# Weight pieces first in the schedule, and three pieces of VectorE's and GpSimd's work moved, in a hybrid block in float32

## The chip, the cores and the metric

The kernel runs on one core of one Trainium2 chip. The metric is the device time of one execution in microseconds, as a median of several; less is better. The core has five engines that matter here, each with its own instructions in a fixed order: TensorE (PE in the profile, PEld for its weight loads), VectorE (DVE), ScalarE (ACT), GpSimd (POOL) and SyncE (SP), which issues most DMAs.

## What is computed

One layer of a decoder block with two branches, for a sequence of 512 and a width of 1024:

```python
u = rmsnorm(x, norm1_g)
proj = u @ w_in       # conv channels of A, z, decay and beta; q, k, v of B; indexer; two gates
# A: gated delta rule, 8 heads, chunks of 64
g = -exp(a_log) * softplus(g_a + dt_bias)
q, k, v = silu(causal conv of width 4 over the channels); q, k normalised
T = inverse of (I + strictly lower (beta k k^T * decay));  then a loop over chunks with a state
# B: the indexer chooses 128 keys a query, 8 query heads attend to them
score = sum over 8 heads of iw * relu(iq . ik)       # causal
o = attention over the top 128 keys
m = sigmoid(gate_a) * A + sigmoid(gate_b) * B
h = x + m @ w_out
h = h + (silu(conv3(up_gate)) * conv3(up_val)) @ w_down     # up: 1024 to 2 x 2816
out = rmsnorm(h, final_g)
```

All inputs are float32.

## The kernel before

The large products are made of float32 parts. A weight comes in pieces of 512 KB ([128, 1024]) by `load`, from SP's queue into `raw`; `piece` then lets ScalarE cast it to the high part `whi` (line 196) and lets VectorE or GpSimd, as its argument says, subtract that from `raw` for the low part `wlo` (line 197). `raw`, `whi` and `wlo` have three buffers each. A product is three matmuls a step (`passes`, lines 200 to 206): high by low, low by high, high by high. Activations are split in the same way (`xgh` and `xgl`, `uTh` and `uTl`, `hTh` and `hTl`). Products are gathered in `acc`, a PSUM tile with three buffers; `channel_major` makes two of them, of 24 matmuls of 512 columns each, from two pieces. Its first argument is the engine for the first piece's low part, its third (GpSimd unless given) that for the second's.

The stages in order of time:

1. dv and the small products (decay, beta, indexer key and weights), from x times g; the row statistics `r4` come from the x tiles `xt`.
2. The indexer's queries: two calls of `channel_major` over `xg` give four accumulators, each cut in two halves; ScalarE copies a half to `iq` and VectorE subtracts it from the accumulator for the low half (line 432). In the meantime VectorE makes the indexer's key `ikn`, the decay chain (lines 383 to 397: `s0`, `s1`, `s2`, `gd`, all 128x32) and `uv`, the normalised x, with its low part `uTl` (lines 420 to 422). The chain's end `gd` is read by a cumulative sum on TensorE (`gp`, line 400).
3. Scores of query blocks 1 to 3, and the first half of branch A (`gdn_half(0)`: 4 heads): convolutions (`conv_silu`: ScalarE makes `y` out of an accumulator, three VectorE rows of line 462 add the shifted ones), the matrices `MT`, and the inverse. The inverse of the 32x32 blocks is a chain on VectorE: 30 steps of two rows, `tw` and `wi` (lines 585 and 587). Its result goes by DMA through memory back to `MT`, is transposed to `UT` (line 597), and products `m1` to `m4` (from line 603) join the blocks.
4. The top-k of each block on VectorE: 16 passes of MAX8 (line 690) and a replacement of the eight found (line 691) over 256, 384 and 512 columns; nothing but VectorE works at it, and its result is wanted by the attention in stage 6.
5. dk, dq, and the second half of branch A (`gdn_half(1)`).
6. Attention, z and the gates, W_out, the feed-forward: 22 chunks of two pieces, whose accumulators are read by ScalarE and twice by VectorE each (lines 896 and 898), then down and the last norm.

Nothing of this order is binding: the framework's scheduler writes every engine's instructions in an order of its own, by priority (the place in the program, unless code changes it) and by simulated readiness. `after(b, a)` makes it place b behind a, without a semaphore.

Of the kernel before, what the change touches and what calls it, by code (L numbers as in the profile page):

```python
# [9 lines left out]
F = mybir.dt.float32  # L10
# [3 lines left out]
OP = mybir.AluOpType  # L14
# [6 lines left out]
NT = S // 128  # L21
# [65 lines left out]
def hybrid_block(ctx: ExitStack, tc: tile.TileContext, x: bass.AP, xc: bass.AP, wp: bass.AP,  # L87
                 chan: bass.AP, rows: bass.AP, out: bass.AP):
    nc = tc.nc
    V, A, P, T = nc.vector, nc.scalar, nc.gpsimd, nc.tensor  # L90
# [5 lines left out]
    def acc(name="acc"):  # L96
        return psum.tile([128, 512], F, name=name, tag="acc", bufs=3)

    def tp(name="tp"):
        return psum.tile([128, 512], F, name=name, tag="tp", bufs=2)  # L100
# [4 lines left out]
    def rec(name="rec"):  # L105
        return psum.tile([128, 512], F, name=name, tag="rec", bufs=2)
# [20 lines left out]
    def after(ins, before):  # L127

        tc.add_manual_dep(ins.ins, before.ins.name,
                          mybir.DependencyInfo(mybir.DependencyClass.NoSync, mybir.DependencyReason.DATA),  # L130
                          reason="order")
        return ins
# [51 lines left out]
    def load(parts=1):  # L184
        raw = pipe.tile([128, 1024], F, name="raw", bufs=3)
        n = 1024 // parts
        for k in range(parts):
            nc.sync.dma_start(raw[:, n * k:n * k + n], wp[pos[0]][:, n * k:n * k + n])
        pos[0] += 1
        hi = pipe.tile([128, 1024], R, name="whi", bufs=3)  # L190
        lo = pipe.tile([128, 1024], R, name="wlo", bufs=3)
        return raw, hi, lo

    def piece(lo_engine):
        raw, hi, lo = load()
        A.copy(hi, raw)  # L196
        lo_engine.tensor_sub(lo, raw, hi.bitcast(F))  # L197
        return hi, lo

    def passes(o, lhs, rhs, first, last, shared=False):  # L200


        (lh, ll), (rh, rl) = lhs, rhs
        a = T.matmul(o, lh, rl, start=first, stop=False, skip_group_check=shared)  # L204
        T.matmul(o, ll, rh, start=False, stop=False, skip_group_check=shared)  # L205
        return a, T.matmul(o, lh, rh, start=False, stop=last, skip_group_check=shared)  # L206

    def cols(pc, k, n, c0, c1):
        return tuple(w.rearrange("p (k c) -> p k c", c=n)[:, k, c0:c1] for w in pc)

    const.tile([128, 16], F, name="pad0")
    uTh = const.tile([128, KT, S], R, name="uTh", tag="uTh")
    uTl = const.tile([128, KT, S], R, name="uTl", tag="uTl")
# [8 lines left out]
    xg = [tuple(sl.tile([128, S], R, name=n, bufs=KT) for n in ("xgh", "xgl")) for _ in range(KT)]  # L222
# [71 lines left out]
    def token_major(eng):  # L294

        pcs = [piece(eng), piece(eng)]
        ps = [acc().rearrange("p (t c) -> p t c", c=256) for _ in range(2)]
        for i in range(2):
            for tb in range(NT):
                for k in range(4):  # L300
                    kk = 4 * i + k
                    passes(ps[tb // 2][:, tb % 2], u_blk(kk, tb), cols(pcs[i], k, 256, 0, 256),
                           kk == 0 and tb % 2 == 0, kk == KT - 1, shared=True)
        return ps

    def channel_major(eng, src=None, second=P):
        pcs = [piece(eng), piece(second)]
        ps = [acc(), acc()]
        for i, pc in enumerate(pcs):
            for t in range(2):  # L310
                for k in range(4):
                    kk = 4 * i + k
                    passes(ps[t], cols(pc, k, 256, 128 * t, 128 * t + 128),
                           src[kk] if src else (uTh[:, kk], uTl[:, kk]), kk == 0, kk == KT - 1)
        return ps
# [53 lines left out]
    def sc8(name):  # L369
        return const.tile([128, NT, H], F, name=name)  # L370

    def b8(ap):
        return ap.unsqueeze(1).to_broadcast([128, NT, H])

    beta, gd, G, GL, eG, dl = (sc8(n) for n in ("beta", "gd", "G", "GL", "eG", "dl"))
    s0, s1, s2 = sc8("s0"), sc8("s1"), sc8("s2")
# [3 lines left out]
    na = const.tile([128, H], F, name="na")  # L380
# [2 lines left out]
    V.tensor_add(s0, sm[:, :, 64:72], b8(dtb))  # L383
    V.scalar_tensor_tensor(s1, s0, -1.0, s0, op0=OP.mult, op1=OP.min)
    A.activation(s1, s1, AF.Exp)
    V.tensor_scalar(s2, s1, 2.0, None, op0=OP.add)
    V.reciprocal(s2, s2)
    V.tensor_mul(s1, s1, s2)
    V.tensor_mul(s2, s1, s1)
    V.tensor_scalar(gd, s2, 1.0 / 17, 1.0 / 15, op0=OP.mult, op1=OP.add)  # L390
    for c in (13, 11, 9, 7, 5, 3, 1):
        V.tensor_mul(gd, gd, s2)
        V.tensor_scalar(gd, gd, 1.0 / c, None, op0=OP.add)
    V.tensor_mul(gd, gd, s1)
    V.tensor_scalar(s0, s0, 0.0, None, op0=OP.max)
    V.scalar_tensor_tensor(gd, gd, 2.0, s0, op0=OP.mult, op1=OP.add)
    V.tensor_mul(gd, gd, b8(na))
    gp = tp("gp")
    g2 = gd.rearrange("p t h -> p (t h)")
    T.matmul(gp[:, 0:32], triu, g2, start=True, stop=True)  # L400
# [17 lines left out]
    for k in range(KT):  # L418
        uv = sl.tile([128, 512], F, name="uv", bufs=3)
        V.scalar_tensor_tensor(uv, xT[k], g1[:, k:k + 1], rB, op0=OP.mult, op1=OP.mult)  # L420
        A.copy(uTh[:, k], uv)
        (V, P)[k % 2].tensor_sub(uTl[:, k], uv, uTh[:, k].bitcast(F))


    iq = []
    for j in range(2):
        for p in channel_major(P, xg):
            for s in range(2):
                q = PR.tile([128, 512], R, name="iq", tag="dqo", bufs=9)
                src = p[64 * s:64 * s + 64]  # L430
                A.copy(q[0:64], src)
                V.tensor_sub(q[64:128], src, q[0:64].bitcast(F))
                iq.append(q)
# [5 lines left out]
    score = {}  # L439
    for b in range(1, NT):  # L440
        n = 128 * (b + 1)
        score[b] = mask[:, m_off[b]:m_off[b] + n]
        for h in range(H):
            p = tp("rel")[:, :n]
            T.matmul(p, iq[h][:, 128 * b:128 * b + 128], ikh[:, :n], start=True, stop=False)
            T.matmul(p, iq[h][:, 128 * b:128 * b + 128], ikl[:, :n], start=False, stop=True)
            w = iw[:, b, h:h + 1]
# [19 lines left out]
        return dst  # L467

    oA = []

    def gdn_half(hh):
        hs = slice(HH * hh, HH * hh + HH)
# [47 lines left out]
        for c in range(NT):  # L520
# [10 lines left out]
            for h2 in range(2):  # L531
                p = rec("kk").rearrange("p (h a i) -> p h a i", h=2, a=2)
# [4 lines left out]
                for i in range(2):  # L537
                    h = 2 * h2 + i
                    V.scalar_tensor_tensor(MT[:, c, h], p[:, i, 0], mk[:, c, h:h + 1], ge[:, 1, h],
                                           op0=OP.mult, op1=OP.mult)  # L540
# [34 lines left out]
        wi = PL.tile([128, 16, 32], F, name="wi", tag="g4", bufs=2)  # L575
# [6 lines left out]
        for j in range(1, 31):  # L582
            m, c = 31 - j, (j + 1) // 2
            w = tw[:, :c * m].rearrange("p (r i) -> p r i", i=m)
            V.tensor_mul(w, wi[:, 0:c, j:j + 1].to_broadcast([128, c, m]),  # L585
                         nn[:, j:j + 1, j + 1:].to_broadcast([128, c, m]))
            V.tensor_sub(wi[:, 0:c, j + 1:], wi[:, 0:c, j + 1:], w)  # L587
        for g in range(2):
            A.dma_start(blv[:, g:32:2], wi[64 * g:64 * g + 64])
        for b in range(4):  # L590
# [39 lines left out]
        for c in range(NT):  # L630
            cs = slice(128 * c, 128 * c + 128)
            g = HH * hh
            if c:
# [3 lines left out]
                for h in range(HH):  # L637
                    V.scalar_tensor_tensor(vt[:, c, h], ps[:, h], neG[:, c, g + h:g + h + 1], vt[:, c, h],
                                           op0=OP.mult, op1=OP.add)
# [14 lines left out]
            if c + 1 < NT:  # L654
                if c:
                    for h in range(HH):
                        V.scalar_tensor_tensor(St[:, h], St[:, h], dl[:, c, g + h:g + h + 1], pu[:, h],
                                               op0=OP.mult, op1=OP.add)
# [15 lines left out]
        for c in range(NT):  # L674
            for h in range(HH):
                V.scalar_tensor_tensor(at[:, c, h], at[:, c, h], f[:, 0, c, h:h + 1], gng,
                                       op0=OP.mult, op1=OP.mult)
        oA.append(at)

    gdn_half(0)  # L680


# [3 lines left out]
    for b in range(1, NT):  # L686
        n = 128 * (b + 1)
        top = const.tile([128, 8], F, name="top", bufs=2)
        for i in range(TOPK // 8):
            V.max(top, score[b])  # L690
            V.match_replace(score[b], top, score[b], TAKEN)  # L691
        V.tensor_scalar(score[b], score[b], -2e38, NEG, op0=OP.is_gt, op1=OP.mult)

# [5 lines left out]
    for j in range(4):  # L699
        for t, p in enumerate(channel_major(P)):  # L700
            q = half_kb("dq")
            A.copy(q, p)
            dq.append(q)

    gdn_half(1)

    oB = []
# [134 lines left out]
    sq2 = PR.tile([128, 256], F, name="sq2", tag="y", bufs=2)  # L842
    for j in range(4):
        pcs = [piece(V), piece(V)]
        if j < 3:
            ps = [acc().rearrange("p (t c) -> p t c", c=256) for _ in range(2)]
# [194 lines left out]
```

## Time and profile before

| | |
|---|---|
| time, median of 3 runs | 965.27 us (964.96 to 965.7) |
| the profiled execution | 966.31 us, its span 964.6 us |
| TensorE busy | 923.5 us, 96% of the span |
| VectorE, ScalarE, GpSimd busy | 603.1, 443.3, 197.6 us |
| chain of work that ended last | TensorE 67%, VectorE 22%, DMA 4%, ScalarE 3% |
| mean DMA rate over the span | 93 GB/s |

The span is the profiled execution from its first to its last instruction. Busy time is the sum of instructions on an engine; TensorE's are pipelined, so a busy TensorE may still be a slow one: the granted clock (PEclk, 1.00 is 2.4 GHz) is read beside it.

### The profile page before, as it was taken

The numbers are of one execution on the slowest core, as the hardware profiler recorded it, in microseconds if no ns is written. First come the engines' busy times: TensorE is split into PE (matmuls) and PEld (weight loads), VectorE is DVE, ScalarE is ACT, GpSimd is POOL, SyncE is SP. The second block draws the span as 40 slices with busy tenths as digits, with TensorE's granted clock in tenths as the row PEclk, the third lists the DMA queues.
The fourth block names the chain that finished last, engine by engine and source line by source line (L and its number), as shares of the span: only waits on it lengthen the run. The fifth ranks groups of instructions, "written<-read, shape, count | busy, mean of one in ns | idle before, by whom it ended". The sixth has DMA issues, their size and how long they took to land.

```text
span 964.6 us, 14658 instructions
## 1 busy us (share of the span) xinstructions
PE 923.5 (96%) x5671; PEld 806.3 (84%) x5671; DVE 603.1 (63%) x1235; ACT 443.3 (46%) x954; POOL 197.6 (20%) x117
## 2 busy tenths in 40 slices
PE   9789999987999998899999999999999999999997
PEld 8668877775887897889999999888888888888886
DVE  6976999896637967756652637556655666522424
ACT  8446864422448844345633436444444444422313
POOL 0644243421110354211235022000000000000201
PEclk9989999997999999999999999999999999999999
DMA  9222221414220222311332222322233232323222
GB/s 325 89 77 99 88 67 65 130 57 110 88 66 2 88 77 70 90 51 50 141 89 95 88 88 90 108 88 96 101 101 97 88 109 87 109 91 106 88 67 88
DMA packets 39830, 89.30 MB, mean 93 GB/s; under 512 B 15664, under 2 KB 16976, under 8 KB 39760
## 3 DMA queue, kind: packets, MB, share of 16 engines
q1 hardware_dynamic: 24192, 81.91, 25.7%
q10 hardware_dynamic: 15568, 6.45, 2.7%
q8 instruction: 45, 0.74, 0.3%
q14 instruction: 25, 0.20, 0.1%
HBM read 85.18 MB, written 3.16 MB: 92 GB/s over the span
## 4 chain that ended last, share of the span: by engine, by line
PE 67%; DVE 22%; DMA 4%; ACT 3%; issue 2%; ACTq 1%; POOL 0%; DVEq 0%; POOLq 0%
PE acc L204 17%; PE acc L206 17%; PE acc L205 17%; PE d L205 3%; PE d L206 3%; PE d L204 3%; DVE wi L587 2%; DVE y L462 2%; DVE tw L585 2%; DVE mask L691 2%; DMA raw<-in_wp_dram 2%; DVE top L690 2%; PE lg L730 1%; PE lg L712 1%; DVE mask L452 1%
## 5 line engine op out<-in xcount | busy, mean ns | idle before, releaser
L196 ACT CAST whi<-raw 128x1024 fp32r<-128x1024 f32 x136 | 142.6, 1049 | 191.4 <-PE acc L206 80.0
L197 POOL TENSOR_TENSOR wlo<-raw,whi 128x1024 fp32r<-128x1024 f32 x60 | 144.7, 2415 | 305.3 <-ACT whi L196 278.3
L197 DVE TENSOR_TENSOR wlo<-raw,whi 128x1024 fp32r<-128x1024 f32 x76 | 94.4, 1242 | 151.3 <-ACT whi L196 151.3
L205 PE MATMUL acc<-hTh,wlo 128*128 128x512 f32 (+1 forms) x368 | 139.8, 380 | 0.0
L204 PE MATMUL acc<-hTl,whi 128*128 128x512 f32 (+1 forms) x368 | 139.1, 381 | 0.2 <-DVE hTl L839 0.2
L206 PE MATMUL acc<-hTh,whi 128*128 128x512 f32 (+1 forms) x368 | 138.8, 380 | 0.0
L205 PE MATMUL acc<-uTh,wlo 128*128 128x512 f32 x272 | 109.8, 404 | 5.1 <-DVE wlo L197 5.1
L204 PE MATMUL acc<-wlo,uTh 128*128 128x256 f32 x384 | 112.0, 292 | 1.6 <-DVE rk_sc L140 1.6
L204 PE MATMUL acc<-uTl,whi 128*128 128x512 f32 x272 | 109.6, 405 | 4.1 <-DVE y L462 3.8
L206 PE MATMUL acc<-whi,uTh 128*128 128x256 f32 x384 | 112.0, 292 | 0.0
L205 PE MATMUL acc<-whi,uTl 128*128 128x256 f32 x384 | 111.9, 291 | 0.0
L206 PE MATMUL acc<-uTh,whi 128*128 128x512 f32 x272 | 109.6, 403 | 0.0
L898 DVE SCALAR_TENSOR_TENSOR fy<-acc,ch,fy 128x511 f32<-128x511 f32 x88 | 65.8, 748 | 26.2 <-ACT fy L896 24.7
L204 PEld LDWEIGHTS acc<-hTl,whi 128*128 128x128 f32 x368 | 69.2, 188 | 13.4 <-DVE hTl L839 0.4
L205 PEld LDWEIGHTS acc<-hTh,wlo 128*128 128x128 f32 x368 | 69.2, 188 | 13.1
L206 PEld LDWEIGHTS acc<-hTh,whi 128*128 128x128 f32 x368 | 69.2, 188 | 13.1
L981 POOL TENSOR_TENSOR h<-h,gf 128x512 f32<-128x512 f32 (+1 forms) x8 | 10.6, 1344 | 338.6 <-ACT sq L977 338.6
L204 PEld LDWEIGHTS acc<-wlo,uTh 128*128 128x128 f32 x384 | 73.3, 191 | 3.3 <-ACT y L460 1.8
L205 PEld LDWEIGHTS acc<-whi,uTl 128*128 128x128 f32 x384 | 73.3, 191 | 1.4 <-issue 1.0
L206 PEld LDWEIGHTS acc<-whi,uTh 128*128 128x128 f32 x384 | 73.2, 191 | 1.4 <-issue 0.7
L204 PEld LDWEIGHTS acc<-uTl,whi 128*128 128x128 f32 x272 | 52.5, 193 | 16.1 <-issue 3.4
L205 PEld LDWEIGHTS acc<-uTh,wlo 128*128 128x128 f32 x272 | 52.8, 194 | 15.6 <-DVE wlo L197 5.5
(310 smaller groups left out, 1906.4 us busy)
## 6 DMA issues: line engine op xcount, KB each, us to landing
raw<-in_wp_dram SPq DMA_DIRECT2D x137, 512.0 KB, 3.5
xT<-in_xc_dram SPq DMA_DIRECT2D x8, 256.0 KB, 5.3
xt<-in_x_dram SPq DMA_DIRECT2D x4, 512.0 KB, 8.1
ge<-gdr ACTq DMA_DIRECT2D x8, 256.0 KB, 3.2
h<-in_x_dram SPq DMA_DIRECT2D x4, 512.0 KB, 6.0
out_dram<-h SPq DMA_DIRECT2D x8, 256.0 KB, 2.2
raw<-in_wp_dram SPq DMA_DIRECT2D x4, 256.0 KB, 4.4
gbias<-in_rows_dram ACTq DMA_DIRECT2D x8, 128.0 KB, 3.2
```

What stands on the lines that cost most here:

```text
L196: A.copy(hi, raw)
L197: lo_engine.tensor_sub(lo, raw, hi.bitcast(F))
L204: a = T.matmul(o, lh, rl, start=first, stop=False, skip_group_check=shared)
L205: T.matmul(o, ll, rh, start=False, stop=False, skip_group_check=shared)
L206: return a, T.matmul(o, lh, rh, start=False, stop=last, skip_group_check=shared)
L462: V.scalar_tensor_tensor(y[:, s:], p[:, :512 - s], cw[:, ti, 3 - s:4 - s], y[:, s:], op0=OP.mult, op1=OP.add)
L585: V.tensor_mul(w, wi[:, 0:c, j:j + 1].to_broadcast([128, c, m]), nn[:, j:j + 1, j + 1:].to_broadcast([128, c, m]))
L587: V.tensor_sub(wi[:, 0:c, j + 1:], wi[:, 0:c, j + 1:], w)
L690: V.max(top, score[b])
L691: V.match_replace(score[b], top, score[b], TAKEN)
L898: V.scalar_tensor_tensor(y[:, s:], p[:, :512 - s], fw[:, ti, 2 - s:3 - s], y[:, s:], op0=OP.mult, op1=OP.add)
L981: P.tensor_mul(hv, hv, gf[:, 512 * half + c.start:512 * half + c.stop])
```

## The change

Five things are changed. `piece` is put under `tc.high_priority(offset=2000)`, so that the scheduler takes a weight's load, cast and subtraction before other work that is ready. The decay chain from line 386 on goes to GpSimd, but for the reciprocal and the maximum; its `scalar_tensor_tensor` becomes two operations, so 21 VectorE rows become 22 of GpSimd. All eight low parts of `u` are made on VectorE, where GpSimd made every second one. The indexer's four pieces get their low parts from VectorE, not GpSimd. The inverse's steps are kept in a list, and the first MAX of the last top-k block is placed behind the last step of the first half's inverse. What is computed stays the same.

```diff
     def piece(lo_engine):
-        raw, hi, lo = load()
-        A.copy(hi, raw)
-        lo_engine.tensor_sub(lo, raw, hi.bitcast(F))
+        with tc.high_priority(offset=2000):
+            raw, hi, lo = load()
+            A.copy(hi, raw)
+            lo_engine.tensor_sub(lo, raw, hi.bitcast(F))
...
-    V.tensor_scalar(s2, s1, 2.0, None, op0=OP.add)
+    P.tensor_scalar(s2, s1, 2.0, None, op0=OP.add)
     V.reciprocal(s2, s2)
-    V.tensor_mul(s1, s1, s2)
+    P.tensor_mul(s1, s1, s2)
...
     for c in (13, 11, 9, 7, 5, 3, 1):
-        V.tensor_mul(gd, gd, s2)
-        V.tensor_scalar(gd, gd, 1.0 / c, None, op0=OP.add)
-    V.tensor_mul(gd, gd, s1)
+        P.tensor_mul(gd, gd, s2)
+        P.tensor_scalar(gd, gd, 1.0 / c, None, op0=OP.add)
+    P.tensor_mul(gd, gd, s1)
     V.tensor_scalar(s0, s0, 0.0, None, op0=OP.max)
-    V.scalar_tensor_tensor(gd, gd, 2.0, s0, op0=OP.mult, op1=OP.add)
-    V.tensor_mul(gd, gd, b8(na))
+    P.tensor_scalar(gd, gd, 2.0, None, op0=OP.mult)
+    P.tensor_add(gd, gd, s0)
+    P.tensor_mul(gd, gd, b8(na))
...
-        (V, P)[k % 2].tensor_sub(uTl[:, k], uv, uTh[:, k].bitcast(F))
+        V.tensor_sub(uTl[:, k], uv, uTh[:, k].bitcast(F))
...
-        for p in channel_major(P, xg):
+        for p in channel_major(V, xg, V):
...
     oA = []
+    tri = []
...
-            V.tensor_sub(wi[:, 0:c, j + 1:], wi[:, 0:c, j + 1:], w)
+            tri.append(V.tensor_sub(wi[:, 0:c, j + 1:], wi[:, 0:c, j + 1:], w))
...
         for i in range(TOPK // 8):
-            V.max(top, score[b])
+            t = V.max(top, score[b])
+            if b == NT - 1 and i == 0:
+                after(t, tri[-1])
             V.match_replace(score[b], top, score[b], TAKEN)
```

Three places of the order show how instructions move. The line numbers of the changed kernel are 2 to 5 higher than those of before (up to 6 at the end).

VectorE, around the first two subtractions for the indexer's queries (`iq`), before:

```order
L432 TENSOR_TENSOR iq<-acc,iq 64x512
L420 SCALAR_TENSOR_TENSOR uv<-xT,ch,rB 128x512
L355 SCALAR_TENSOR_TENSOR ikn<-ikn,rik_sc,rv 128x64 x4
L393 TENSOR_SCALAR gd<-gd 128x32
L422 TENSOR_TENSOR uTl<-uv,uTh 128x512
L420 SCALAR_TENSOR_TENSOR uv<-xT,ch,rB 128x512
L432 TENSOR_TENSOR iq<-acc,iq 64x512
```

and now:

```order
L199 TENSOR_TENSOR wlo<-raw,whi 128x1024
L435 TENSOR_TENSOR iq<-acc,iq 64x512
L283 COPY rB<-rp 128x512
L341 TENSOR_TENSOR sm<-smp,r_177 128x512
L423 SCALAR_TENSOR_TENSOR uv<-xT,ch,rB 128x512 x3
L435 TENSOR_TENSOR iq<-acc,iq 64x512
```

Between the two subtractions stood rows of the key `ikn`, of `u` and one of the decay chain (`gd`); now there are the broadcast `rB`, the small products `sm` and three `uv`. A piece's low part (`wlo`) stands ahead of them.

GpSimd, from its first piece on, before:

```order
L197 TENSOR_TENSOR wlo<-raw,whi 128x1024 x4
L422 TENSOR_TENSOR uTl<-uv,uTh 128x512 x2
L197 TENSOR_TENSOR wlo<-raw,whi 128x1024
L422 TENSOR_TENSOR uTl<-uv,uTh 128x512 x2
L197 TENSOR_TENSOR wlo<-raw,whi 128x1024 x3
```

and now (the first part; 11 more rows of the chain follow behind the third piece):

```order
L199 TENSOR_TENSOR wlo<-raw,whi 128x1024
L388 TENSOR_SCALAR s_450<-s_449 128x32
L390 TENSOR_TENSOR s_449<-s_449,s_450 128x32
L391 TENSOR_TENSOR s_450<-s_449 128x32
L199 TENSOR_TENSOR wlo<-raw,whi 128x1024
L392 TENSOR_SCALAR gd<-s_450 128x32
L394 TENSOR_TENSOR gd<-gd,s_450 128x32
L395 TENSOR_SCALAR gd<-gd 128x32
L394 TENSOR_TENSOR gd<-gd,s_450 128x32
L395 TENSOR_SCALAR gd<-gd 128x32
L394 TENSOR_TENSOR gd<-gd,s_450 128x32
L395 TENSOR_SCALAR gd<-gd 128x32
```

The four indexer pieces and the low parts of `u` are gone from here; the decay chain stands between the pieces for dq and the convolutions.

VectorE at the end of the first half's inverse, before:

```order
L587 TENSOR_TENSOR wi<-wi,tw 128x15x2
L585 TENSOR_TENSOR tw<-wi,nn 128x15
L587 TENSOR_TENSOR wi<-wi,tw 128x15
L595 MEMSET UT 32x16x32
L597 STREAM_TRANSPOSE UT<-MT 32x16x32 x3
L197 TENSOR_TENSOR wlo<-raw,whi 128x1024
L462 SCALAR_TENSOR_TENSOR y<-acc,cw,y 128x511
L462 SCALAR_TENSOR_TENSOR y<-acc,cw,y 128x510
```

and now:

```order
L591 TENSOR_TENSOR wi<-wi,tw 128x15x2
L589 TENSOR_TENSOR tw<-wi,nn 128x15
L591 TENSOR_TENSOR wi<-wi,tw 128x15
L599 MEMSET UT 32x16x32
L694 MAX top<-mask 128x8
L697 MATCH_REPLACE mask<-top,mask 128x512
L694 MAX top<-mask 128x8
L697 MATCH_REPLACE mask<-top,mask 128x512
L694 MAX top<-mask 128x8
L697 MATCH_REPLACE mask<-top,mask 128x512
L601 STREAM_TRANSPOSE UT<-MT 32x16x32
L694 MAX top<-mask 128x8
```

The passes of the last top-k block, which stood among the steps of the inverse and before it, now follow its last step; the transposes of `UT`, the next piece's low part and the convolution's rows (`y`, line 465 now) come between them and behind them. On TensorE the first product with `UT` moves from place 899 of the order to place 840.

On SP's queue the first indexer piece's load now stands ahead of the four loads of `xt`. In the feed-forward the second piece's cast and subtraction stand ahead of the reading of the other accumulator.

## Rows read from the trace of the kernel before

**Rows 1.** page, part 1: engine, busy us (share of the span), instructions
```profile
PE 923.5 (96%) x5671; PEld 806.3 (84%) x5671; DVE 603.1 (63%) x1235; ACT 443.3 (46%) x954; POOL 197.6 (20%) x117
```

**Rows 2.** windows: stretch, length, busy (x) PE PEld DVE ACT POOL, PEclk, DMA, GB/s
```profile
24.00:73.00 49.00, 40.73 (x164) 32.06 (x165) 40.53 (x82) 19.59 (x34) 25.96 (x12) 0.90 0.27 86
73.00:209.00 136.00, 132.56 (x642) 109.47 (x641) 123.31 (x292) 76.45 (x197) 55.00 (x32) 1.00 0.28 88
209.00:262.00 53.00, 44.46 (x367) 35.17 (x366) 35.45 (x70) 14.75 (x23) 8.04 (x4) 0.90 0.29 86
```

**Rows 3.** waits of PE, 24 to 73 us: total us, times, longest
```profile
PE acc L204 <- DVE iq L432: 4.4, 2, 4.1
PE gp L400 <- DVE gd L397: 3.0, 1, 3.0
```

**Rows 4.** waits of PE, 209 to 262 us, same columns
```profile
PE acc L205 <- DVE wlo L197: 5.1, 1, 5.1
...
PE m L603 <- DVE UT L597: 0.9, 1, 0.9
```

**Rows 5.** timeline of PE: start, us, engine line op out<-in [idle before <-releaser]
```profile
213.49 0.39 PE L206 MATMUL acc<-uTh,whi 128*128 128x512 f32 x1
213.72 0.39 PE L204 MATMUL acc<-uTl,whi 128*128 128x512 f32 x1
219.16 0.79 PE L205 MATMUL acc<-uTh,wlo 128*128 128x512 f32 x1 [5.05 <-DVE wlo L197]
219.75 0.63 PE L206 MATMUL acc<-uTh,whi 128*128 128x512 f32 x1
220.18 0.63 PE L204 MATMUL acc<-uTl,whi 128*128 128x512 f32 x1
```

**Rows 6.** timelines of POOL and DVE, 23 to 182 us, same columns
```profile
23.94 7.08 POOL L197 TENSOR_TENSOR wlo<-raw,whi 128x1024 fp32r<-128x1024 f32 x3 [1.51 <-ACT whi L196]
...
28.64 2.43 DVE L383 TENSOR_TENSOR s<-sm,rv 128x32 f32<-128x32 f32 x1
...
35.78 0.18 DVE L393 TENSOR_SCALAR gd<-gd 128x32 f32<-128x32 f32 x1
...
180.93 2.55 POOL L197 TENSOR_TENSOR wlo<-raw,whi 128x1024 fp32r<-128x1024 f32 x1 [8.08 <-ACT whi L196]
...
181.14 0.68 DVE L690 MAX8 top<-mask 128x8 f32<-128x512 f32 x1
```

**Rows 7.** timelines of DVE and POOL; line 197: ns min/median/max, first and last start
```profile
43.92 0.69 DVE L422 TENSOR_TENSOR uTl<-uv,uTh 128x512 fp32r<-128x512 f32 x1
...
59.74 2.26 DVE L397 TENSOR_TENSOR gd<-gd,na 128x32 f32<-128x32 f32 x1
...
20.06 0.53 POOL L289 TENSOR_SCALAR gng<-rv 128x128 f32<-128x128 f32 x1 [15.34 <-DMA rv<-in_rows_dram]
...
L197 DVE TENSOR_TENSOR wlo<-raw,whi x76: 1214/1225/2066, 217.9 to 942.5; 128x1024 fp32r<-128x1024 f32 x76
L197 POOL TENSOR_TENSOR wlo<-raw,whi x60: 2342/2398/2807, 23.9 to 607.0; 128x1024 fp32r<-128x1024 f32 x60
```

**Rows 8.** page, part 6, DMA issues: count, KB each, median us to landing
```profile
raw<-in_wp_dram SPq DMA_DIRECT2D x137, 512.0 KB, 3.5
```

**Rows 9.** lines by form, DVE, 182 to 212 us: busy us, mean ns
```profile
L691 DVE MATCH_REPLACE8 mask<-top,mask 128x512 f32<-128x512 f32 x10 | 6.7, 670 | 0.0
L690 DVE MAX8 top<-mask 128x8 f32<-128x512 f32 x9 | 6.1, 682 | 0.0
```

**Rows 10.** timelines of ACT, DVE and PE in the feed-forward, 641 to 653 us
```profile
641.40 0.78 ACT L896 ACTIVATE fy<-acc,ch 128x512 f32<-128x512 f32 x1 [1.94 <-PE acc L206]
642.08 1.04 ACT L196 CAST whi<-raw 128x1024 fp32r<-128x1024 f32 x1
...
642.21 1.53 DVE L898 SCALAR_TENSOR_TENSOR fy<-acc,ch,fy 128x511 f32<-128x511 f32 x2 [0.91 <-ACT fy L896]
...
652.30 0.39 PE L205 MATMUL acc<-hTh,wlo 128*128 128x512 f32 x1
```

More of the change, by code (lines that the diff above doesn't have):

```diff
@@ L385, in hybrid_block @@
     A.activation(s1, s1, AF.Exp)
-    V.tensor_scalar(s2, s1, 2.0, None, op0=OP.add)
+    P.tensor_scalar(s2, s1, 2.0, None, op0=OP.add)
     V.reciprocal(s2, s2)
-    V.tensor_mul(s1, s1, s2)
-    V.tensor_mul(s2, s1, s1)
-    V.tensor_scalar(gd, s2, 1.0 / 17, 1.0 / 15, op0=OP.mult, op1=OP.add)
+    P.tensor_mul(s1, s1, s2)
+    P.tensor_mul(s2, s1, s1)
+    P.tensor_scalar(gd, s2, 1.0 / 17, 1.0 / 15, op0=OP.mult, op1=OP.add)
     for c in (13, 11, 9, 7, 5, 3, 1):
-        V.tensor_mul(gd, gd, s2)
-        V.tensor_scalar(gd, gd, 1.0 / c, None, op0=OP.add)
-    V.tensor_mul(gd, gd, s1)
+        P.tensor_mul(gd, gd, s2)
+        P.tensor_scalar(gd, gd, 1.0 / c, None, op0=OP.add)
+    P.tensor_mul(gd, gd, s1)
     V.tensor_scalar(s0, s0, 0.0, None, op0=OP.max)
-    V.scalar_tensor_tensor(gd, gd, 2.0, s0, op0=OP.mult, op1=OP.add)
-    V.tensor_mul(gd, gd, b8(na))
+    P.tensor_scalar(gd, gd, 2.0, None, op0=OP.mult)
+    P.tensor_add(gd, gd, s0)
+    P.tensor_mul(gd, gd, b8(na))
     gp = tp("gp")
```

## The prediction

> **What bounds the kernel now.** The page comes first: TensorE is busy for 923.5 of 964.6 us [rows 1], so only what keeps it from its work, or slows it, can move the end. The windows by stage say where that is [rows 2]. A busy sum hides a second loss, the granted clock, so each window is read twice: 24 to 73 us has 49.00 - 40.73 = 8.3 us of idle time and a mean clock of 0.90; 209 to 262 has 53.00 - 44.46 = 8.5 us and again 0.90; 73 to 209, between them, loses 3.4 us at full clock.
>
> The waits view names the causes. In the first window it is `iq` of line 432 (4.4 us) and `gd` of line 397 (3.0 us) [rows 3]: two products of VectorE. In the second it is a weight's low part from VectorE, 5.1 us in one wait, and, less, the transposed `UT` [rows 4]. TensorE's timeline then shows what a long wait leaves behind [rows 5]: from 213.72 to 219.16 nothing starts, and the matmuls after it start 0.59 and then 0.43 us apart (219.16, 219.75, 220.18). The pitch before is 0.227 us (213.49 to 213.72). So the engine comes out of a 5 us wait at the lower clock level, 1.2 GHz; with 8 to 12 matmuls at that pace a long wait costs some 2 us more than it shows.
>
> VectorE's and GpSimd's timelines tell why VectorE is late [rows 6]. A 128x32 addition starts at 28.64 and takes 2.43 us; GpSimd's three pieces begin at 23.94 and end at 31.02. The addition ends at 31.07, with the GpSimd row. The same operations without such a neighbour take 0.18 us. MAX8, which starts at 181.14 under a GpSimd piece (180.93 to 183.48), takes its usual 0.68. So a VectorE row with two operands in SBUF may be held to the end of a GpSimd row that runs beside it.
>
> **Part by part.** The sum is made against the profiled execution's 966.3 us, 1.0 above the median.
>
> *First window: pieces first, four low parts and four of u to VectorE, decay chain to GpSimd.* TensorE's own work there is 144 matmuls of 512 columns (96 of the indexer, 48 of u) at 0.227 us, 32.7 us, and some 3 us of small ones, against 49; so about 13 us are idle time and low clock. To VectorE come 4 pieces of 1.22 and 4 rows of 0.69 us (7.6 us); from it go 21 rows of the chain, 0.18 us each where nothing holds them, the last 2.26 [rows 6, 7]; held ones counted, I put them at about as much. Its load stays; the order changes. Today a subtraction for `iq` comes 4.1 us late for TensorE [rows 3], behind rows of `u`, `ikn` and the decay chain; now five rows stand between the first two, no decay row among them, and GpSimd has no indexer piece beside them. I count VectorE's rows from the first to the last of the eight subtractions at 22 us, beside 28 us of matmuls, so TensorE should no longer wait for them, except at the first.
> Price of the chain on GpSimd: no row of before has a 128x32 operation there. Bounds: VectorE's own 0.18 us for such a row [rows 6], and GpSimd's 0.53 for 128x128 [rows 7]. From 0.53 for 128 and 2.40 for 1024 elements per partition comes the estimate 0.53 - 96 x 0.0021 = 0.33 us, which I take, as the nearest engine's. 22 rows are 7.3 us, with the bounds 4.0 to 11.7; three pieces of 2.40 stand among them. Starting near 39 us (the sum at line 383, 28.64 today, now follows two `iq` subtractions, three `uv` and a piece), `gd` is ready at 39 + 7.2 + 7.3 + about 2 for the turns with VectorE = 55.5, at worst 60. `gp`, at 62.05 today with 3.0 and 4.4 us of waits ahead of it (some of it made up elsewhere), is wanted near 58.6 then. So the 3.0 us wait goes, without a new one over 1.3.
> New costs: three GpSimd pieces can each hold a VectorE row for up to 2.3 us, and one 512 KB weight piece now goes ahead of the four x tiles on SP's queue, so the statistics come up to 3.5 us later, its median landing [rows 8]; I take 1 us for the load and 2 for the holding. 13 - 3 gives **-10**, bounds -13 (all back) and 0 (the waits form again).
>
> *Middle, 73 to 209.* Some five passes of the last top-k block stood here; each is 0.68 + 0.67 us less overlap, 1.28. 6.4 us of VectorE's work leave, 3.4 us of idle time are there [rows 2]: **-2**, bounds -3.4 and 0.
>
> *Second window.* In 182 to 212 us, 9 MAX8 and 10 replacements stood inside the inverse: 6.1 + 6.7 = 12.8 us [rows 9]. They go behind its last step, and of six inverse rows that GpSimd pieces held there, each up to 2.25 us over its length as in rows 6, some may be free, as the pieces' places shift; I count three, 5 us. The order puts the first product with UT 59 TensorE rows earlier (899 to 840), 13.4 us at 0.227. The inverse comes earlier by about as much as it is needed earlier; the wait stays near 0.9 to 1.6 us [rows 4]. Behind it VectorE now has the passes (16 x 1.28 = 20.5 us), with the transposes, two pieces and copies among them. Up to the convolution's `y` that frees an accumulator I count 12 MAX and 11 replacements (14.7 us), some 10 us of the others and 2.2 of its own rows, 26.7 us, beside some 24 us of TensorE's rows until it wants that buffer (106 at 0.227). That is a new wait of 2.6 us, with 0.7 for a transpose queued behind a pass and one or two held rows. In all about 7 of the present 8.5 + 0.10 x 53 = 14 us come back: **-7**, bounds -11 and +2 (both waits as long as today's, with the low clock after each).
>
> *The rest.* The second inverse (300 to 425) keeps its order in the main; the feed-forward's second piece per chunk is cast and subtracted ahead of the other accumulator's evacuation. That is 1.04 + 1.22 us; the accumulator is read at 641.40 to 643.74 and TensorE comes back to its buffer near 652.3 [rows 10], 8.6 us later, so it is covered. Nor does a row of these stretches leave. **0**, bounds -3 (held rows of the second inverse, as in the first) and 0.
>
> Sum: -10 - 2 - 7 = -19: 947.3 for a profiled execution, **946.3** for the median.
>
> **A rule that speaks against it.** What rows 6 show, a 0.18 us row lasting 2.43 us until GpSimd's ends, is the case that the Trainium skill describes in "SBUF — State Buffer", section "Who interferes with whom": the two engines share a port pair, held for a whole instruction, and a VectorE instruction with two SBUF inputs contends. The trace agrees, and with it that MAX8 isn't held. The skill's "GPSIMD Engine Reference", section "4.1 Engine selection", would leave two-input elementwise work on VectorE, as GpSimd is about half as fast; the trace agrees for pieces (2.40 against 1.22 us). By that page the decay chain is on the wrong engine; the first rival below is what that would cost.
>
> **Rivals.**
> 1. *The decay chain becomes late.* It decides once a GpSimd row takes more than (58.6 - 39 - 7.2 - 2) / 22 = 0.47 us, dependent rows and their waits included. At 0.95 us `gd` is ready near 67, TensorE waits 8.5 us and leaves at low clock (2 us): the first window gives nothing, and the sum is some -9: 956. Against it: the 0.33 from rows 7; for it: 22 rows that each wait for the one before, which no row of before shows on GpSimd. 0.14.
> 2. *Behind the inverse the waits form again.* The passes delay transposes or convolutions by 5 us instead of 2.6, twice, each with low clock: the second window's 7 go, and two more: near 956. For it: VectorE's and TensorE's counts are only 2.6 us apart. 0.14.
> 3. *Slower: the feed-forward turns.* If the piece put ahead closes a ring (the evacuation waits for a cast that waits for a weight buffer that the accumulator's matmuls must free), each of 22 chunks waits. It decides when the evacuation is put off by more than 8.6 us, and outdoes the gain from 19 / 22 = 0.9 us per chunk; at 1.2 us the time is 966.3 - 19 + 26.4 - 1 = 973. Against it: the added work is a quarter of the slack. 0.07.
> 4. *More comes back than I count*: no new wait in the first window, no held rows, the second inverse also gains: -13 - 3 - 10 - 1 = -27, 938. 0.1.
>
> **How the numbers follow.** The forecast (941 to 953) has 0.55. With rivals 1, 2 and 4 the range is **937 to 960**; outside lie rival 3 and the worst of 1 with 2 together. 0.2% (1.9 us) is about what a measurement of this kernel can tell from no change. Faster by more than it: the forecast, 1, 2 and 4 nearly whole, 0.89; within it 0.03, where rivals 1 and 2 meet; slower 0.08, rival 3 and a little.
>
> **What would show it.** Right: the first window shorter by some 10 us at a clock near 1.0, no wait for `iq` above 1 us, `gp` without a wait; between the inverse and the first convolution behind it one or two waits under 3 us; the feed-forward's length unchanged. Wrong: `gp` waiting for GpSimd's `gd` (1), waits of 5 us for UT or `y` with 0.43 us pitches behind them (2), any wait for `fy` that recurs every 10.9 us (3).

## The result and the profile after

| | before | after |
|---|---|---|
| median | 965.12 us (4 runs, 964.72 to 965.7) | 950.92 us (4 runs, 950.79 to 951.2) |
| profiled execution, span | 966.31, 964.6 us | 950.98, 949.2 us |
| TensorE busy | 923.5 us, 96% | 920.1 us, 97% |

The ratio is 0.9857, 95% interval 0.9842 to 0.9872: 14.2 us faster. The forecast was 946.3, its range 937 to 960. The sign and the range held, and the gain is three quarters of the 19 us forecast.

Where it came from can be read without choosing windows. TensorE runs the same 5671 rows in both kernels; counted along its timeline, at some points the same rows have been done (or all but a dozen), and the difference between the two times there is what has been gained so far:

```
rows done   before us   after us   gain so far   stage that ends there
  311         72.78       65.81       7.0        first window
  731        160.72      151.29       9.4        
  911        199.66      190.54       9.1        middle
 1464        287.71      272.31      15.4        second window
 3494        539.28      523.98      15.3        second half, attention, gates
 5654        955.73      940.41      15.3        feed-forward, down, norm
```

So the first window gave 7.0, the middle 2.1, the second window 6.3 and the rest nothing; in the feed-forward the difference stays at 15.32 row after row. (These are the two profiled executions, 15.3 us apart; the medians are 14.2 apart.) The middle's gain comes before 160 us of the kernel before; from there to 200 us, where the first passes of the last top-k block stood, nothing is gained.

The windows by stage after the change (columns as in [rows 2], the bounds moved with the stages):

```profile
24.00:64.00 40.00, 36.45 (x153) 29.17 (x152) 35.18 (x62) 19.13 (x31) 17.17 (x26) 0.91 0.27 86
64.00:200.00 136.00, 131.31 (x646) 109.40 (x644) 119.78 (x297) 74.75 (x197) 56.05 (x33) 1.00 0.29 90
200.00:250.00 50.00, 46.38 (x398) 38.27 (x399) 43.08 (x78) 22.46 (x46) 8.39 (x5) 0.93 0.28 90
```

Against [rows 2], idle time in the first window falls from 8.3 to 3.6 us, but the clock stays low, 0.91. In the third it falls from 8.5 to 3.6, clock 0.93. So both windows still hold a long wait. TensorE's waits view, 24 to 64 us and then 200 to 250 us, in the columns of [rows 3, 4]:

```profile
PE acc L206 <- DVE uTl L425: 3.6, 2, 2.1
```

```profile
PE m L607 <- DVE UT L601: 5.2, 2, 3.8
```

In the view of [rows 4] a second wait stands between the two that are shown there:

```profile
PE acc L204 <- DVE y L462: 2.5, 1, 2.5
```

The waits of [rows 3] for `iq` and `gd` are gone, and so are those of the kernel before for a weight's low part and, but for 0.2 us, for `y`. In their place stand two for `uTl`, of 3.6 us together, and two longer ones for `UT`, 5.2 us where it was 0.9 (the first begins at 198.4, 1.6 us ahead of the window).

Why `uTl` is late is in the timelines of VectorE and GpSimd after the change (columns as in [rows 6]); the third fence, TensorE's, has the second of the two waits and what follows it:

```profile
45.66 2.30 DVE L352 TENSOR_TENSOR ikn<-ikn 128x256 f32<-128x256 f32 x1
...
52.20 2.33 DVE L354 TENSOR_SCALAR lnst<-lnst 128x4 f32<-128x4 f32 x1
...
54.64 0.70 DVE L425 TENSOR_TENSOR uTl<-uv,uTh 128x512 fp32r<-128x512 f32 x1
```

```profile
45.28 2.40 POOL L199 TENSOR_TENSOR wlo<-raw,whi 128x1024 fp32r<-128x1024 f32 x1
...
51.63 2.87 POOL L199 TENSOR_TENSOR wlo<-raw,whi 128x1024 fp32r<-128x1024 f32 x1
...
58.42 0.25 POOL L400 TENSOR_TENSOR gd<-gd,na 128x32 f32<-128x32 f32 x1
```

```profile
55.40 0.80 PE L206 MATMUL acc<-uTl,whi 128*128 128x512 f32 x1 [2.09 <-DVE uTl L425]
55.99 0.63 PE L207 MATMUL acc<-uTh,wlo 128*128 128x512 f32 x1
56.42 0.63 PE L208 MATMUL acc<-uTh,whi 128*128 128x512 f32 x1
```

A row over 128x4 starts at 52.20 and ends at 54.53, with the GpSimd piece (51.63 + 2.87 = 54.50); `uTl` stands behind it. TensorE comes out of the wait at the lower clock level: eleven matmuls, from 55.99 to 60.26, start 0.43 us apart instead of 0.227, some 2 us more. The decay chain on GpSimd is ready at 58.7, and `gp` runs at 65.78 without a wait.

### The profile page after: what moved, and what is told of

Its sections match the earlier page's. It is cut to its first block, busy times and chain, and to the rows that moved or that the text cites. A ratio compares the mean times of both kernels' runs of the same rounds, so it can differ in the third digit from the quotient of the medians.

```text
span 949.2 us, 14678 instructions
## 1 busy us (share of the span) xinstructions
PE 920.1 (97%) x5671; PEld 807.0 (85%) x5671; DVE 601.7 (63%) x1222; ACT 442.9 (47%) x954; POOL 193.3 (20%) x131
## 4 chain that ended last, share of the span: by engine, by line
PE 72%; DVE 18%; DMA 3%; issue 2%; ACT 2%; POOL 1%; ACTq 0%; DVEq 0%; POOLq 0%
PE acc L206 19%; PE acc L207 18%; PE acc L208 18%; PE d L207 3%; PE d L208 3%; PE d L206 3%; DVE tw L589 2%; DVE wi L591 2%; DVE y L465 2%; PE lg L718 1%; DVE mask L697 1%; PE lg L736 1%; DMA MT<-bl 1%; DVE top L694 1%; DMA nn<-bl 1%
## 5 line engine op out<-in xcount | busy, mean ns | idle before, releaser
L199 DVE TENSOR_TENSOR wlo<-raw,whi 128x1024 fp32r<-128x1024 f32 x80 | 99.7, 1247 | 158.8 <-ACT whi L198 158.6
L199 POOL TENSOR_TENSOR wlo<-raw,whi 128x1024 fp32r<-128x1024 f32 x56 | 139.0, 2484 | 294.4 <-ACT whi L198 260.3
L208 PEld LDWEIGHTS acc<-uTh,whi 128*128 128x128 f32 x272 | 52.1, 191 | 10.5
```

## The experiments

Ratios are to the kernel before, run on the same chip beside them (its median was 965.1, 966.8 and 965.9 us in the three groups of four), with 95% intervals; the change itself has 0.9857 (0.9842 to 0.9872). Single runs of one kernel lay up to some 5 us apart there, so differences of two or three microseconds are read from the stages of the profiles and not from a median alone. The gains by stage are made in the way of the table above, the first window's at 81 to 99 us, where these kernels' orders agree (the change has 7.0 to 7.2 there). A profile is one execution too: the change and a kernel below (the product with `UT` later) have the same order on all engines up to 190 us, and by then their gains differ by 2.1 us.

**Parts left out.** First the priority:

```diff
-        with tc.high_priority(offset=2000):
-            raw, hi, lo = load()
-            A.copy(hi, raw)
-            lo_engine.tensor_sub(lo, raw, hi.bitcast(F))
+        raw, hi, lo = load()
+        A.copy(hi, raw)
+        lo_engine.tensor_sub(lo, raw, hi.bitcast(F))
```

> The changed kernel without the priority for the weight pieces; all else as changed. Theory (the gain is 7.0 us in the first window, mostly from who computes what; 2 in the middle; 6.3 behind the inverse from the order of the top-k): the priority only brings the first indexer pieces forward, so 2 to 3 us of the first window are lost, 953 to 954. Rival (the priority carries the first window): 957 to 958, with a wait for iq of 4 us back. If the priority gave nothing: 951.

948.09 us, 0.9817 (0.9791 to 0.9843): not slower at all; if anything faster, the intervals just touch. The first window gave 6.7 (7.2 with the priority): what the priority brings forward is worth 1.1 us at 32 us and 0.5 at 81, no more than two executions can differ by. A wait of 2.1 us for `iq` is back, those for `uTl` are gone. The theory fell. Up to 288 us this kernel is 3 us behind the change, and then it passes it: from 286 to 410 us its clock is 1.00 where the changed kernel has 0.97, which waits there for the second half's `UT` (2.9 us) with the low clock behind. That the priority causes this isn't shown: from 288 us to the end of the gates this kernel gains 6.7 us on the kernel before, and three others without the priority, below, gain 3.6, 3.0 and -0.4.

The decay chain back on VectorE (the 22 GpSimd rows replaced by the 21 of before):

```diff
...
-        P.tensor_mul(gd, gd, s2)
-        P.tensor_scalar(gd, gd, 1.0 / c, None, op0=OP.add)
+        V.tensor_mul(gd, gd, s2)
+        V.tensor_scalar(gd, gd, 1.0 / c, None, op0=OP.add)
...
```

> The changed kernel with the decay chain back on VectorE, 21 rows. Theory (VectorE is late in the first window, and rows of the chain that GpSimd's pieces hold make it later): the waits for uTl grow from 3.6 to 6 us or more and gp waits again; 3 to 5 us lost, 954 to 956. Rival (a chain of small two-input rows is on the wrong engine on GpSimd): gd ready no later, VectorE loses only 4 us of short rows that fit its gaps, and the time stays at 951 or falls to 949.

949.96 us, 0.9841 (0.9814 to 0.9868): the same as the change. The wait for `uTl` is 2.7 us instead of 3.6, the one for `gp` 0.3, and the first window gave 8.1 where the change gave 7.2. So the rival was right: no worth of the chain's move can be seen here. VectorE's rows of it are 0.18 us long; GpSimd's are twice as long, and TensorE waits for neither by more than 0.3 us.

The last top-k block free of its rule:

```diff
             if b == NT - 1 and i == 0:
-                after(t, tri[-1])
+                pass
```

> The changed kernel without the rule that puts the last top-k block behind the inverse. Theory (the 6.3 us of the second window come from it): the passes stand between the inverse's steps again, 16 before its end, and waits for a weight's low part or for y are back; 956 to 958. Rival (the first product with UT stands later in TensorE's order without it, at 909 in place of 840, so that the later inverse isn't waited for): 950 to 952.

957.85 us, 0.9922 (0.9895 to 0.995): 6 to 7 us lost. The first window and the middle gave 8.2, the second window nothing (7.9 at its end). The middle alone gave 2.0, as with the rule. TensorE's waits, 190 to 262 us:

```profile
PE acc L207 <- DVE wlo L199: 5.5, 1, 5.5
PE m L607 <- DVE UT L601: 3.7, 1, 3.7
```

The 5.1 us wait of [rows 4] is back, in the same place: a piece's subtraction that stands among the inverse's steps. The theory held.

The low parts back on GpSimd:

```diff
-        V.tensor_sub(uTl[:, k], uv, uTh[:, k].bitcast(F))
+        (V, P)[k % 2].tensor_sub(uTl[:, k], uv, uTh[:, k].bitcast(F))
...
-        for p in channel_major(V, xg, V):
+        for p in channel_major(P, xg):
```

> The changed kernel with the low parts of the four indexer pieces, and of every second u, back on GpSimd. Theory (GpSimd pieces of 2.4 us hold VectorE's rows and delay the chain that now shares GpSimd): the first window loses most of its 7.0 us, 956 to 958, with iq or gd waited for. Rival (VectorE's own load bounds the first window, and 7.6 us less of it helps): 948 to 951.

954.81 us, 0.9886 (0.9865 to 0.9908): 3 to 4 us lost. The first window gave only 2.4, and `iq` is waited for, 8.6 us in two waits. Ahead of the longer one, of 6.1 us, stand two held rows, in the timelines of VectorE, GpSimd and TensorE:

```profile
53.25 2.27 DVE L140 TENSOR_TENSOR rik_sc<-rik_sc,lnst 128x4 f32<-128x4 f32 x1
...
55.76 2.26 DVE L139 SCALAR_TENSOR_TENSOR rik_sc<-rik_sc 128x4 f32<-128x4 f32 x1
58.05 0.69 DVE L435 TENSOR_TENSOR iq<-acc,iq 64x512 fp32r<-64x512 f32 x1
...
53.16 2.34 POOL L199 TENSOR_TENSOR wlo<-raw,whi 128x1024 fp32r<-128x1024 f32 x1
...
55.66 2.34 POOL L199 TENSOR_TENSOR wlo<-raw,whi 128x1024 fp32r<-128x1024 f32 x1
...
58.89 0.77 PE L206 MATMUL acc<-uTl,whi 128*128 128x512 f32 x1 [6.08 <-DVE iq L435]
```

Both end with a GpSimd piece, and the subtraction for `iq` comes behind them. So 5 of the first window's 7 us are these low parts. Further on the lead grows much as in the change, to 5.8 at 200 us and 9.6 at 287. The theory held for the place; its time was 1 to 3 us too high.

**Parts alone**, each by its lines of the change's diff, on the kernel before. The priority:

> The kernel before with nothing but the priority for the weight pieces. Theory (the priority brings the first pieces 1 to 2 us forward and costs 3 to 5 us from 300 us on, as the run without it showed): 965 to 968, no faster than before. Rival (it brings a gain by itself, which the other parts take away): 958 to 962.

963.11 us, 0.9963 (0.9951 to 0.9975): 3.6 us faster. The theory fell here too: alone the priority does help. Its profiled execution is the fastest of seven, 959.23 us: it gained 3.4 us in the first window, 2.0 in the middle and 1.7 from there on, so how the median's 3.6 us divide isn't shown. Nor is it shown why the priority helps alone and not beside the other parts.

The last top-k block behind the inverse:

> The kernel before with nothing but the last top-k block behind the inverse. Theory (this part alone gives the second window's 6 to 7 us, as the run without it lost 6.9): 957 to 960, the first window as before, with its waits for iq and gd. Rival (it pays only where the first window has been shortened): 963 to 966.

956.64 us, 0.9903 (0.9882 to 0.9924). The first window gave 1.1, another 1.6 came between 160 and 180 us, where passes of the block had stood, and the rest from 200 us on; the single wait left there is `UT`, 6.7 us. The theory held, and its time was a little too high: this part is the largest, and it needs none of the others.

**What was left in the changed kernel.** The first half's four key pieces on VectorE as well, so that no GpSimd piece runs beside VectorE's rows in the first window until 61.0 us:

```diff
-            for t, p in enumerate(channel_major(P, second=V if hh else P)):
+            for t, p in enumerate(channel_major(P if hh else V, second=V)):
                 conv_silu(p, 8 + HH * hh + 2 * j + t, kT[:, 2 * j + t])
```

> The changed kernel with the low parts of the first half's four key pieces on VectorE too, so that no 2.4 us row of GpSimd runs beside VectorE in the first window. Theory (the 3.6 us of waits for uTl and the low clock behind them come from two VectorE rows held 2.2 us each by those pieces): the waits for uTl fall under 1 us, the first window gains 3 to 5 us more, 946 to 948. Rival (VectorE's load makes uTl late, and 4 x 1.22 us more of it makes it later): waits for uTl of 5 us or more, 952 to 955.

949.83 us, 0.9818 (0.9795 to 0.984). The two rows that were held, in this kernel's VectorE timeline:

```profile
45.27 0.43 DVE L352 TENSOR_TENSOR ikn<-ikn 128x256 f32<-128x256 f32 x1
45.62 1.28 DVE L199 TENSOR_TENSOR wlo<-raw,whi 128x1024 fp32r<-128x1024 f32 x1
...
50.53 1.27 DVE L199 TENSOR_TENSOR wlo<-raw,whi 128x1024 fp32r<-128x1024 f32 x1
...
52.34 0.21 DVE L354 TENSOR_SCALAR lnst<-lnst 128x4 f32<-128x4 f32 x1
```

They take 0.43 and 0.21 us, and the pieces 1.28 where GpSimd took 2.40. TensorE waits 1.1 us for `uTl` in place of 3.6, and the windows view of 24 to 66 us shows the clock at full speed:

```profile
24.00:66.00 42.00, 40.95 (x189) 33.51 (x188) 36.95 (x73) 22.66 (x38) 12.62 (x24) 1.00 0.34 103
```

At 93 us this kernel is 11.3 us ahead of before, the change 7.2 (two more kernels with this edit, below, have 11.7 and 11.1 there; the six others that keep the low parts on VectorE, but not this edit, have 6 to 8). So the pieces beside VectorE cost the first window 4 us: this is shown. By 200 us the lead over the change is down to 0.5 us, behind waits of 2.0 us in the scores and 1.8 at `kk`, and then 5.8 us for `UT` in one wait, where the change's longest is 3.8. By the ratio it is 3.8 us faster than the change, by the medians 1.1; its profiled execution, the slowest of its four runs, ends 0.6 ahead. The place was right, and most of what is won there is lost to later waits.

The first product with `UT` later in TensorE's order: the first of its matmuls is placed behind a step of the second half's first product (the list `steps` keeps the passes of the last `channel_major`).

```diff
...
-            for t, p in enumerate(channel_major(P, second=V if hh else P)):
+            ps = channel_major(P, second=V if hh else P)
+            if hh and not j:
+                after(m1[0], steps[7][1])
+            for t, p in enumerate(ps):
...
```

> The changed kernel with the first product with UT placed 28 TensorE rows (6.3 us) later, behind the eighth step of the second half's first product. Theory (the 5.2 us wait for UT is TensorE coming too early, while the inverse's data are on their way through memory): the wait falls to about 0 and the low clock behind it goes, 5 to 7 us gained by the time the next product ends, but only what isn't lost further on stays: 945 to 948. Rival (the inverse's chain of products and the state loop behind it set the second half, so a later product only moves the wait): 950 to 952.

949.11 us, 0.9813 (0.979 to 0.9836). Its waits from 190 to 262 us:

```profile
PE m L621 <- DVE yt L617: 3.1, 1, 3.1
PE acc L207 <- POOL wlo L199: 0.9, 1, 0.9
```

The wait for `UT` is gone; the next product of the inverse's chain now waits, 3.1 us, for VectorE's copy `yt`, which stands among the top-k passes. From 911 rows to 1458 this kernel gained 6.4, the change 6.2 to 1466: the wait moved by one step and little was won. What its profile gained more than the change, it had by then: 2.1 us, before 200 us, where the two kernels' orders are alike; that is a difference between two runs. The rival named what happens, the next product's wait; the time, 949.11, lies between the two ranges, and by the ratio, on the scale of the change's runs, it is 947.1, in the theory's.

**Together.** Pairs and triples of these edits; in the last two the product with `UT` stands four steps later still:

```diff
-                after(m1[0], steps[7][1])
+                after(m1[0], steps[11][1])
```

The priority left out and the chain on VectorE:

> The changed kernel without the priority and with the decay chain on VectorE: only the low parts' engines and the place of the last top-k block are left of the change. Theory (each of the two left-out parts costs 1 to 3 us by itself, and they act in different stages: the chain in the first window, the priority from 300 us on): 945 to 948. Rival (both hang on the same order of VectorE's rows): 949 to 952.

948.3 us, 0.9807 (0.9778 to 0.9835): between the two ranges, by the ratio (946.5) in the theory's.

The priority left out and the product with `UT` later (`steps[7]`):

> The changed kernel without the priority and with the first product with UT 29 TensorE rows later. Theory (the priority's cost from 300 us on and the early product's wait are separate): both gains add, 943 to 946. Rival (both free the same time in the second half): 947 to 949.

950.78 us, 0.9844 (0.9824 to 0.9863): above both ranges.

The key pieces on VectorE and the product later (`steps[11]`):

> The changed kernel with the first half's key pieces on VectorE and the first product with UT behind the twelfth step of the second half's first product. Theory (the held rows cost 4 us in the first window, the early product 2 to 3 in the second, in separate places): 943 to 946. Rival (TensorE, earlier by 4 us, waits for the inverse's products instead): 947 to 949.

948.44 us, 0.9825 (0.9804 to 0.9846): the rival's time.

The same, with the priority left out:

> The same with the priority left out as well. Theory (three separate losses taken away): 940 to 944. Rival (the priority is needed where VectorE makes still more low parts, since their subtractions then stand behind other work): 946 to 950.

951.35 us, 0.9848 (0.9828 to 0.9869): above both ranges. The gains don't add in the last three. The third kernel shows one reason. At 200 us it is 12.4 us ahead of before, and the first half's wait for `UT` is gone; yet from there to 287 us it gains 6.4, no more than the change. For TensorE now waits 5.3 us for ScalarE's copy of `dq` out of an accumulator. ScalarE's timeline in this kernel, with its DMA issues (ACTq):

```profile
186.19 0.58 ACT L715 COPY dq<-acc 128x512 f32<-128x512 f32 x1
197.83 1.30 ACTq L600 DMA_DIRECT2D bl<-wi  x2
201.46 0.31 ACTq L602 DMA_DIRECT2D MT<-bl  x1
201.89 1.04 ACT L198 CAST whi<-raw 128x1024 fp32r<-128x1024 f32 x1 [15.12 <-DMA bl<-wi]
201.91 1.48 ACTq L602 DMA_DIRECT2D MT<-bl  x3
203.43 0.59 ACT L715 COPY dq<-acc 128x512 f32<-128x512 f32 x1 [0.50 <-issue]
```

The DMAs that store the inverse and read it back are issued by ScalarE. They stand in its order ahead of a cast and a copy; the first waits for VectorE's last step (197.83) and the second for the store to land (201.46), and nothing of ScalarE's runs for 15.1 us. In the changed kernel a cast waits in the same place for 10.0 us, and in the kernel before one follows 18.7 us of idle time there. A kernel with these issues on another queue wasn't tried.

Of the best kernels, the change without the priority and with the chain on VectorE (0.9807, upper bound 0.9835), the one with the product later (0.9813, 0.9836) and the one with the key pieces on VectorE (0.9818, 0.984) are ahead of the change (lower bound 0.9842) by their ratios, by some 4 us; they can't be told apart from each other. The change wasn't run beside them, and the kernel before was 1.7 us slower there than beside the change: as measured, their medians are 1.1 to 2.6 us below the change's 950.92. So how far ahead they are stays open.

## Why the prediction was right, and by how much it was off

- *What bounds the kernel*: right. The gain is TensorE's idle time and low clock in the two windows that the windows view pointed out, and nothing from 288 us on.
- *First window, -10*: -7.0. **This is the step that was mis-sized.** The waits for `iq` and `gd` went, and the decay chain's price came out near the estimate (0.34 and 0.41 us a row on average, with one and two inputs, estimated at 0.33; `gd` ready at 58.7, forecast 55.5, wanted only at 65.8). But the term for new costs had 2 us for all the VectorE rows that GpSimd's pieces hold. VectorE took 28.6 us from the first to the last of the eight subtractions, put at 22: three held rows (2.39, 2.30 and 2.33 us) are some 6 us of the difference. TensorE paid 3.6 us of waits and some 2 of low clock: the matmuls behind the second wait ran at the lower level, the very thing that the prediction had read in [rows 5] for the waits that went, and had not charged to those that came. With the holding taken away 11.3 us had come by 93 us.
- *The rule against it*. The holding, which the trace showed in [rows 6], is the mechanism that the Trainium skill gives in "SBUF — State Buffer", section "Who interferes with whom"; the run with the key pieces on VectorE agrees, 2.30 and 2.33 us against 0.43 and 0.21 for the same rows. The second of them has one input in SBUF, where the prediction, from [rows 6], named rows with two. For the chain, the rule of "GPSIMD Engine Reference", section "4.1 Engine selection", agrees in the durations (0.41 us a two-input row against VectorE's 0.18) but not in a price: with the chain on VectorE the time was the same.
- *Middle, -2*: -2.1, by luck. The term was five passes that leave VectorE; where they stood, from 160 us on, nothing was gained, and the kernel without the top-k's rule gained 2.0 in the middle as well. The rule alone gained 1.6 there. Two executions of one order differ by as much, so where the 2.1 us come from stays open.
- *Second window, -7*: -6.3, but by other waits. Forecast were 0.9 to 1.6 us for `UT` and 2.6 for `y`; there are 5.2 and about 0.2. The prediction set TensorE's 59 rows against VectorE's work that leaves and left out that the 5.05 us wait for the low part, and the low clock behind it, stood *ahead* of that product and went with it. So TensorE wants the product 30.4 us earlier (198.4, where it was 228.8), and the inverse's last step ends 27.4 earlier (195.64, where it was 223.07). The data come back from memory at 201.5 and 204.6 (VectorE's transposes wait for `MT` until then). That the sum came near is partly luck: the longer wait for `UT` stands in for the one for `y`.
- *The rest, 0*: 0.1 lost in all, with 1 to 2 us gained and given back on the way. The feed-forward's slack held: the difference between the kernels doesn't change by 0.01 us over it, so rival 3 is out.
- *Rivals 1 and 4* are out as well: `gp` doesn't wait, and there were new waits. (At rival 1's 0.95 us a row its own sum gives 69, not the 67 that it names; nothing hangs on it.) *Rival 2* is half there, in the 5.2 us for `UT` with the low clock behind it, but it took only a part of the 14 us.
- *The parts*: the top-k's place is worth 6 to 9 us (left out, alone), the low parts on VectorE 3 to 4; the chain nothing that can be seen. The priority is worth 3.6 us alone, and in the presence of the others nothing or a little less than nothing; which of the two, the intervals leave open.

## What to carry to other kernels

Charge a new wait in the same currency as the one that it replaces: length and what the clock does after it. When a wait ahead of an instruction goes, everything behind it comes earlier by that much, and what was just in time becomes the next wait: here much of each further gain was met by the inverse's trip through memory. Work for an engine that nothing waits for (the top-k) belongs behind the chain that something waits for; that one rule was about half of the gain.

## What the runs showed that was not expected

- DMA issues that wait held the engine that issues them. ScalarE stood for 15.1 us behind the storing and reading back of the inverse (10.0 in the changed kernel, 18.7 in the kernel before), with a cast and a copy behind it, and TensorE then waited 5.3 us for one of those copies.
- A row with one operand in SBUF was held as well: `lnst` times a constant, 128x4, took 2.33 us beside a GpSimd piece and 0.21 without.
- Gains don't add: three edits of the changed kernel gave about 4 us each by their ratios, in different stages, and no pair or triple of them gave more.
